# Second attention layer of a hybrid decoder step: 33 steps of one or two units, products ordered by shape

## The chip, the cores and the metric

The kernel runs on one core of one Trainium2 chip. The time of a kernel is the device time of one execution in microseconds; the figure used is the median over several runs. A profiled execution gives a page and a trace; its time is one single value and is told beside its span.

The engines named below are TensorE (PE; loading of its weights is listed as PEld), VectorE (DVE), ScalarE (ACT), GpSimd (POOL) and SyncE (SP). Every large load of the part that is changed is issued by SP, in one queue and in the order in which the instructions stand there.

## The reference

One inference step of a small decoder with two layers: a prompt of 512 positions and eight sequences of four new positions each. All is float32.

```python
D_MODEL = 1024; SEQ = 512; DEC_BATCH = 8; DEC_SEQ = 4; PAST_LEN = 1024
KV_HEADS = 8; ATT_HEAD_DIM = 128
WINDOWS = (128, 512, 2048); DILATIONS = (1, 4, 16)
...
u = rmsnorm(h, g_norm) @ w_in                      # second layer: queries of 3 groups x 8 heads, and the gate
q = u[..., :Q_WIDTH].reshape(b, l, N_DIL_GROUPS, KV_HEADS, ATT_HEAD_DIM)
for g in range(N_DIL_GROUPS):                      # one attention for each dilation group
    o, lse = attend(q[:, :, g], biases[g], DILATIONS[g], WINDOWS[g] // DILATIONS[g])
w = jax.nn.softmax(jnp.stack(lses, axis=0), axis=0)
o = jnp.sum(w[..., None] * jnp.stack(outs, axis=0), axis=0)
y = o.reshape(b, l, ATT_WIDTH) * jax.nn.silu(gate)
return y @ w_out
```

The first layer is a state-space mixer (a projection to 5,152 columns, a short convolution, a scan over chunks of 128 positions, a gate and an output projection). From its result one set of keys and values is projected. The second layer attends with three dilations. The prompt's queries attend within the prompt; the new positions attend to 1,024 cached positions and their own four, with the cached keys and values read from memory. A last norm follows.

## The kernel before, in words

The kernel is one program with five stretches: the first mixer, its output projection with the projection of keys and values, the second layer's attention, the output projection, and the last norm. The attention stretch runs from about 570 us to 875 us of the span, and the change is in it alone.

**Weight products.** A float32 product is made of three products of halves: weights and data are each split into a high and a low part, and high by high, high by low and low by high are summed. In the attention stretch the generator `filler()` hands out weight products one by one: the projection to queries and gates (tiles `pa` and `pb`, from data `bq` and weights `whi` and `wlo`, 128 by 128 weights, 272 columns wide; twelve of them make one block), 1,344 in all, and then those of the output projection. Every one of them uses all 128 columns of TensorE. `run(n)` takes the next n. ACT makes `whi` and DVE makes `wlo` from the loaded `wraw`, three blocks ahead.

**Attention units.** `attend(h, n)` is head h and block n of 128 prompt queries; `sample(h, q)` is head h and four of the eight sequences. Each is a generator, cut by `yield` into stages. There are eight heads with four blocks and two samples each, and `combine()`, which weighs the new positions' three groups.

`attend` has four stages. The first forms scores `sp` in PSUM: eight products with 32 columns for the dilated groups and one full product, then the bias and the exponential on DVE and ACT. The second turns the weights (`ptp`, two or three full transposes) and copies them out (`pt`, `ptz`, on ACT). The third forms `pv`: one or two full products and four with 32 columns; ACT scales it. The fourth turns the result (`op`, one full transpose).

`sample` has three stages. The first loads the bias (`sbt`, four loads, with the head's first sample), loads the cached keys (`kc`, two loads of 640 KB into a tile with two buffers), forms scores `s` from them with products of 32 columns (first `s1`, four products 512 wide, of which the first two read the first load of `kc`; then `s2`), runs the softmax into `ss`, and issues the loads of the cached values (`vc`, two of 640 KB, two buffers). The second loads the new values (`vn`), turns `ss` (`w`: six full transposes into two PSUM tiles) and copies it to `wt` on ACT. The third forms `so`: twenty products of 32 columns with `vc` and four with `vn`.

A load into `kc` waits until the `s` that reads the buffer's former content is done, a load into `vc` until the `so` of the sample before is done. All of these PSUM tiles but `pa` and `pb` share one tag with five buffers (`pss`).

**What sets the order.** The program order of TensorE's instructions is kept as written. The other engines' instructions, SP's loads among them, are put in order by the scheduler, and each engine works its list in that order. The written order of the attention stretch is the loop at lines 1643 to 1668: 49 units in a row. An iteration runs the next stage of units u−4, u−2 and u−3, then starts unit u, then takes 24 weight products (20 from unit 44 on). A unit's stages are thus spread over up to five iterations, with weight products between.

Of the kernel before, what the change touches and what calls it, by code (L numbers as in the profile page):

```python
# [34 lines left out]
ATH = 8  # L35
# [19 lines left out]
OCN, SKIP = 2, 1  # L55
POOL_A = (0, 1, 2, 3)
POOL_B = (0, 1, 2)
PRO, OFF, PACE = 9, 8, (57, 62, 64, 44)
LA, FILL, SLOW = 2, (24, 20), 44
TH = T // 2  # L60


# [65 lines left out]
def tile_yoco_step(  # L128
# [16 lines left out]
    def mm(*a, **k):  # L145
        pin(nc.tensor.matmul(*a, **k))  # L146
# [147 lines left out]
    def dap(t, off, ap):  # L294
        a = t[:]
        return bass.AP(tensor=a.tensor, offset=a.offset + off, ap=ap)
# [617 lines left out]
    live = []  # L914
# [457 lines left out]
    def attend(h, n):  # L1372
        bt, qp = bt_t[h], [qp_t[h, g] for g in range(3)]
        kv = kv_t[h]
        kt = kv[:, 0, :]
        vb, vr = (kv[:, i, 0:SEQ].rearrange("p (n d) -> p n d", n=4) for i in (1, 2))
        kp = kt[:, NS:T]
        ktr = kp.rearrange("p (n r i) -> p r n i", n=4, r=4)
        bt12 = bt[:, 256:512].rearrange("p (a c) -> p a c", a=2)
        w = 32 * (n + 1)  # L1380
        g0 = 128 if n == 0 else 256
        sp = pss("sp")
        k0 = max(0, n - 1) * 128
        for g in range(2):
            for r in range(4):
                mm(sp[32 * r:32 * r + 32, g0 + w * g:g0 + w * g + w],
                   qp[1 + g][:, 128 * n + 32 * r:128 * n + 32 * r + 32], ktr[:, r, 0:n + 1, :], start=True, stop=True)
        mm(sp[:, 0:g0], qp[0][:, 128 * n:128 * n + 128], kp[:, k0:128 * n + 128], start=True, stop=True)
        s_ = wk.tile([128, 512], F32, name="s", bufs=3)
        mx = wk.tile([128, 4], F32, name="mx", bufs=4)  # L1390
        s12 = s_[:, g0:g0 + 2 * w].rearrange("p (a c) -> p a c", a=2)
        nc.vector.tensor_tensor_reduce(out=s12, in0=sp[:, g0:g0 + 2 * w].rearrange("p (a c) -> p a c", a=2),
                                       in1=bt12[:, :, 128 - w:128], scale=1.0, scalar=-3e38,
                                       op0=ALU.add, op1=ALU.max, accum_out=mx[:, 1:2])
        nc.vector.tensor_tensor_reduce(out=s_[:, 0:g0], in0=sp[:, 0:g0], in1=bt[:, 256 - g0:256], scale=1.0,
                                       scalar=-3e38, op0=ALU.add, op1=ALU.max, accum_out=mx[:, 0:1])
        nc.vector.tensor_scalar(mx[:, 2:3], mx[:, 0:1], mx[:, 1:2], -1.0, op0=ALU.max, op1=ALU.mult)
        nc.scalar.activation(s_[:, 0:g0 + 2 * w], s_[:, 0:g0 + 2 * w], AF.Exp, bias=mx[:, 2:3], accum_out=mx[:, 3:4])
        nc.vector.tensor_tensor(s12[:, 0, :], s12[:, 0, :], s12[:, 1, :], op=ALU.add)
        nc.vector.reciprocal(mx[:, 3:4], mx[:, 3:4])  # L1400
        yield
        tp = pss("ptp", (128, 3, 128))
        nk = g0 // 128
        for i in range(nk):
            transpose(tp[:, i, :], s_[:, 128 * i:128 * i + 128], ident)
        transpose(tp[0:w, 2, :], s_[:, g0:g0 + w], ident)
        pt = wk.tile([128, 2, 128], F32, name="pt", bufs=2)
        nc.scalar.copy(pt[:, 0:nk, :], tp[:, 0:nk, :])
        nc.scalar.copy(ptz[n][0:w, :], tp[0:w, 2, :])
        yield  # L1410
        pv = pss("pv")[:, 0:128]
        for i in range(nk):
            b = n - nk + 1 + i
            mm(pv, pt[:, i, :], vb[:, b, :], start=i == 0, stop=False, skip_group_check=True)
        for r in range(4):
            mm(pv[32 * r:32 * r + 32, :], ptz[n][:, 32 * r:32 * r + 32], vr[:, r, :],
               start=False, stop=True, skip_group_check=True)
        on = wk.tile([128, 128], F32, name="on", bufs=1)
        nc.scalar.activation(on, pv, AF.Copy, scale=mx[:, 3:4])
        yield  # L1420
        if h not in op_t:
            op_t[h] = pss("op")
        op = op_t[h]
        transpose(op[:, 128 * n:128 * n + 128], on, ident)
        op_n[h] = op_n.get(h, 0) + 1
        yt = y_t[h // 4][:, h % 4, :]
        if h == 7 and op_n[h] >= 3:
            c0, c1 = ((128, SEQ), (0, 128))[op_n[h] - 3]
            y7 = yt[:, NS + c0:NS + c1]
            assert len(gated) == 2  # L1430
            nc.vector.scalar_tensor_tensor(y7, op[:, c0:c1], 0.5, y7, op0=ALU.mult, op1=ALU.mult)
            y_split(h, NS + c0, NS + c1)
        elif h < 7 and op_n[h] == 4:
            nc.vector.tensor_copy(yt[:, NS:T], op)
            att_done.add(h)
# [5 lines left out]
    def sample(h, q):  # L1441
# [27 lines left out]
        for jp in range(2):  # L1469
            vc.append(wk.tile([128, 2, 5, 128], F32, name="vc", bufs=2))  # L1470
            dma(vc[jp], cv[h, q, :, 2 * jp:2 * jp + 2, :, :])
        yield
        dma(vn[0:TS], dap(vnd, h * 128 + 4 * q * TS * ATH * 128, [[ATH * 128, TS], [TS * ATH * 128, 4], [1, 128]]))
        w1, w2 = pss("w1", (128, 4, 128)), pss("w2", (128, 2, 128))
        for i in range(5):
# [2 lines left out]
        nc.scalar.copy(wt[:, 0:4, :], w1)  # L1478
        nc.scalar.copy(wt[:, 4, :], w2[:, 0, :])
        nc.scalar.copy(wt[0:TS, 5, :], w2[0:TS, 1, :])  # L1480
        yield
        so = pss("so")[:, 0:128]
        for i in range(6):
# [6 lines left out]
    def combine():  # L1490
# [16 lines left out]
        with tc.high_priority():  # L1507
# [7 lines left out]
                nc.vector.tensor_tensor(lgv[:, g], lgv[:, g], sm_, op=ALU.mult)  # L1515
            nc.vector.memset(lt[:, :, 12:32], 0.0)
        yield
        lp2 = pss("lp2")
        transpose(lp2[:, 0:16], lt.rearrange("p a b -> p (a b)"), ident[0:16, 0:16])
        cmw = sbt[:, 0:272].rearrange("p (a b) -> p a b", b=16)  # L1520
        ws, cm = cmw[:, 16, :], cmw[:, 0:16, :]
        with tc.high_priority():
            nc.vector.tensor_copy(ws, lp2[:, 0:16])
            nc.vector.tensor_tensor(cm, sel[:, None, :].to_broadcast([128, 16, 16]), bc(ws, 16), op=ALU.mult)
        yield
        oc = pss("oc", (128, ATH, 2, 16))
        for h in range(ATH):
# [108 lines left out]
    def run(n):  # L1636
        m = min(n, ahead[0]) if n > OCN else 0
        ahead[0] -= m
        for _ in range(n - m):
            if next(fill, 0) == 0:  # L1640
                return

    units = [(f, (h, i)) for h in range(ATH - 1) for f, i in
             ((attend, 0), (sample, 0), (attend, 1), (attend, 2), (sample, 1), (attend, 3))]
    units += [(sample, (7, 0)), (attend, (7, 1)), (attend, (7, 2)), (sample, (7, 1)), (attend, (7, 3)), (combine, ()), (attend, (7, 0))]
    fill = filler()
    fetch_kv(0)
    for _ in range(2 * 84):
        next(fill)
    fetch_kv(1)  # L1650
    live = []
    for u in range(len(units) + LA + 2):
        i = u - LA
        if u == len(units) - 2 + SKIP:
            ahead[0] = ATH * OCN
        for j in (i - 2, i, i - 1):
            if 0 <= j < len(units):
                next(live[j], 0)
        if u < len(units):
            f, a = units[u]  # L1660
            if f is attend and a[0] not in bt_t:
                bt_t[a[0]] = bias_tile(a[0])
            if f is attend and a[1] == 2 and 0 < a[0] < ATH - 1:
                fetch_kv(a[0] + 1)
            live.append(f(*a))
            next(live[u])
        run(FILL[u >= SLOW])
    run(10000)
    bctx.close()

# [94 lines left out]
```

## Time and profile before

| | |
|---|---|
| median of 3 runs | 926.12 us (924.83 to 927.18) |
| profiled execution | 932.11 us, span 930.2 us |
| granted TensorE clock, mean | 0.996 |
| TensorE busy | 908.9 us, 98% of the span |
| VectorE, ScalarE, GpSimd busy | 74%, 53%, 18% |
| attention stretch | about 570 to 875 us of the span |
| cached keys and values | 32 + 32 loads of 640 KB each on SP's queue |

A row of the timeline gives start and length in us, the engine, the line, and what was formed from what; several instructions in a row of one kind are put together, and a product of 32 columns stands in it as `128*32` and counts two records. The start of the next row tells when TensorE took up the next thing; the lengths overlap, since products are pipelined. Numbers after `[` are the idle time just before and what ended it. Line 146 is the helper for all products, line 149 that for all transposes, so groups are told apart by their tiles.

### The profile page before, as it was taken

What the parts mean: (1) busy time and instruction counts of PE and PEld (TensorE: products, weight loads), DVE (VectorE), ACT (ScalarE), POOL (GpSimd) and SP (SyncE); (2) the same over time, 40 slices, a digit from 0 to 9 for tenths busy, and PEclk for the clock granted to TensorE, in tenths of its full rate; (3) what the DMA queues carried; (4) which work ended last, traced back from release to release, by engine and by line L of the source; (5) the groups of instructions that cost most, each with busy time, mean ns of one, the idle gap of its engine ahead of it and who ended that gap; (6) DMA issues with size and microseconds to landing.
All of it is one profiled execution on the core that took longest, in us unless ns stands there. A gap on an engine that the chain in (4) does not pass through costs nothing.

```text
span 930.2 us, 21888 instructions
## 1 busy us (share of the span) xinstructions
PE 908.9 (98%) x8671; PEld 847.9 (91%) x8671; DVE 687.5 (74%) x1435; ACT 489.9 (53%) x1140; POOL 163.0 (18%) x212
## 2 busy tenths in 40 slices
PE   8999999999999999999999999999999999999997
PEld 7989888888989889999999999999899999989997
DVE  6998899989799899644489335876677766778732
ACT  6678655655566655422255213555455555557642
POOL 2031344433514642111101001000000000000021
PEclk9999999999999999999999999999999999999999
DMA  8224365355364442536277556757768868774511
GB/s 295 93 74 155 104 206 166 121 170 170 134 201 161 149 165 101 156 108 228 90 256 227 183 184 196 265 182 264 252 203 262 280 204 267 270 256 155 194 49 49
DMA packets 80573, 168.48 MB, mean 181 GB/s; under 512 B 19990, under 2 KB 37736, under 8 KB 79960
## 3 DMA queue, kind: packets, MB, share of 16 engines
q1 hardware_dynamic: 73784, 154.60, 50.5%
q10 hardware_dynamic: 5616, 9.75, 2.8%
q0 software_dynamic: 1072, 2.74, 1.1%
q8 instruction: 68, 1.11, 0.5%
q14 instruction: 33, 0.27, 0.1%
HBM read 141.14 MB, written 25.93 MB: 180 GB/s over the span
## 4 chain that ended last, share of the span: by engine, by line
PE 82%; DVE 9%; DMA 4%; ACT 2%; issue 2%; POOL 0%; SPq 0%; POOLq 0%; DVEq 0%; ACTq 0%
PE pa L146 33%; PE pb L146 28%; PE sp L146 3%; PE pv L146 2%; PE so L146 2%; PE s L146 2%; DVE wlo L206 2%; DMA kc<-ck 1%; PE yd L146 1%; DMA m<-aed 1%; DVE co L641 1%; PE csp L146 1%; PE w L149 1%; PE ptp L149 1%; PE xp L149 1%
## 5 line engine op out<-in xcount | busy, mean ns | idle before, releaser
L205 ACT ACTIVATE whi<-wraw 128x1024 fp32r<-128x1024 f32 x69 | 72.8, 1056 | 97.0 <-PE pb L146 57.2
L206 DVE TENSOR_TENSOR wlo<-wraw,whi 128x1024 fp32r<-128x1024 f32 x69 | 89.6, 1298 | 45.1 <-ACT whi L205 44.7
L146 PE MATMUL pa<-bq,whi 128*128 128x272 f32 x512 | 103.1, 296 | 0.0
L146 PE MATMUL pb<-nl,whi 128*128 128x288 f32 x280 | 84.0, 300 | 0.0
L146 PE MATMUL pb<-nh,wlo 128*128 128x288 f32 x280 | 83.5, 298 | 0.0
L146 PE MATMUL pb<-nh,whi 128*128 128x288 f32 x280 | 83.4, 298 | 0.0
L146 PEld LDWEIGHTS pa<-bq,whi 128*128 128x128 f32 x512 | 81.2, 189 | 0.9
L146 PE MATMUL pa<-nh,whi 128*128 128x256 f32 x280 | 81.1, 290 | 0.5 <-DVE uz L681 0.5
L146 PE MATMUL pa<-nl,whi 128*128 128x256 f32 x280 | 80.7, 288 | 0.0
L146 PE MATMUL pa<-nh,wlo 128*128 128x256 f32 x280 | 80.1, 286 | 0.0
L146 PE MATMUL pb<-bq,whi 128*128 128x272 f32 x384 | 77.2, 296 | 1.3 <-DVE kv L1230 1.1
L146 PE MATMUL pa<-bq,wlo 128*128 128x272 f32 x256 | 74.2, 290 | 0.0
L641 DVE SCALAR_TENSOR_TENSOR co<-cb,cvp,co 128x568 f32<-128x568 f32 x72 | 64.0, 892 | 1.5 <-ACT co L639 0.9
L146 PEld LDWEIGHTS pb<-bq,whi 128*128 128x128 f32 x384 | 60.8, 189 | 2.6 <-DVE kv L1230 1.3
L1289 ACT ACTIVATE whi<-wraw 128x512 fp32r<-128x512 f32 x64 | 40.1, 627 | 35.2 <-PE pb L146 16.8
L146 PEld LDWEIGHTS pb<-nl,whi 128*128 128x128 f32 x280 | 53.0, 189 | 4.4 <-issue 4.4
L146 PEld LDWEIGHTS pa<-nh,whi 128*128 128x128 f32 x280 | 53.8, 192 | 2.6 <-issue 1.9
L146 PE MATMUL pb<-bq,wlo 128*128 128x272 f32 x192 | 55.5, 289 | 0.0
L146 PEld LDWEIGHTS pa<-nl,whi 128*128 128x128 f32 x280 | 53.8, 192 | 1.4 <-issue 1.4
L146 PEld LDWEIGHTS pb<-nh,wlo 128*128 128x128 f32 x280 | 53.1, 190 | 2.2 <-issue 2.2
L146 PEld LDWEIGHTS pa<-nh,wlo 128*128 128x128 f32 x280 | 53.8, 192 | 0.9 <-issue 0.9
L146 PEld LDWEIGHTS pb<-nh,whi 128*128 128x128 f32 x280 | 53.0, 189 | 0.8 <-issue 0.8
(408 smaller groups left out, 2788.0 us busy)
## 6 DMA issues: line engine op xcount, KB each, us to landing
wraw<-w_in SPq DMA_DIRECT2D x40, 512.0 KB
kc<-ck SPq DMA_DIRECT2D x32, 640.0 KB
vc<-cv SPq DMA_DIRECT2D x32, 640.0 KB
wraw<-wb SPq DMA_DIRECT2D x32, 512.0 KB
s<-s SPq DMA_DIRECT2D x32, 256.0 KB
m<-aed SPq DMA_DIRECT2D x16, 512.0 KB
ssmS<-s ACTq DMA_DIRECT2D x32, 256.0 KB
wraw<-w_out SPq DMA_DIRECT2D x16, 512.0 KB
```

The lines of the kernel that those rows point to most:

```text
L146: pin(nc.tensor.matmul(*a, **k))
L149: pin(nc.tensor.transpose(*a))
L205: a = nc.scalar.activation(hi, raw, AF.Copy)
L206: b = lo_eng.tensor_tensor(lo, raw, f32(hi), op=ALU.subtract)
L641: nc.vector.scalar_tensor_tensor(o, cb[:, k:k + n], cvp[:, ti, k:k + 1], o, op0=ALU.mult, op1=ALU.add)
L1289: nc.scalar.activation(hi, src[p][j], AF.Copy)
```

## The change

The 49 units become 33 steps of one or two units: for each head (first sample, block 0), (block 1), (second sample, block 2), (block 3), and a tail for the last head with `combine` and a last block. Each stage that mixes shapes gets one more `yield`, so that a step can run the full products of several units first, then all products with 32 columns, then the full score products. A step u runs the transposes of step u−4, those of u−2, the full `pv` of u−3, then the 32-column products of u−3 (`so`, `pv`) and of the new step u (`s`, `sp`), then the full `sp`, then 36 weight products (40, 24 and 40 in three late steps, 20 after them). The weight products of a head are 144 in both versions (6 × 24 and 4 × 36).

```diff
@@ -56,7 +56,7 @@
 POOL_A = (0, 1, 2, 3)
 POOL_B = (0, 1, 2)
 PRO, OFF, PACE = 9, 8, (57, 62, 64, 44)
-LA, FILL, SLOW = 2, (24, 20), 44
+LA = 2
 TH = T // 2
 
 
@@ -1385,6 +1385,7 @@
             for r in range(4):
                 mm(sp[32 * r:32 * r + 32, g0 + w * g:g0 + w * g + w],
                    qp[1 + g][:, 128 * n + 32 * r:128 * n + 32 * r + 32], ktr[:, r, 0:n + 1, :], start=True, stop=True)
+        yield
         mm(sp[:, 0:g0], qp[0][:, 128 * n:128 * n + 128], kp[:, k0:128 * n + 128], start=True, stop=True)
         s_ = wk.tile([128, 512], F32, name="s", bufs=3)
         mx = wk.tile([128, 4], F32, name="mx", bufs=4)
@@ -1412,6 +1413,7 @@
         for i in range(nk):
             b = n - nk + 1 + i
             mm(pv, pt[:, i, :], vb[:, b, :], start=i == 0, stop=False, skip_group_check=True)
+        yield
         for r in range(4):
             mm(pv[32 * r:32 * r + 32, :], ptz[n][:, 32 * r:32 * r + 32], vr[:, r, :],
                start=False, stop=True, skip_group_check=True)
@@ -1470,6 +1472,7 @@
             vc.append(wk.tile([128, 2, 5, 128], F32, name="vc", bufs=2))
             dma(vc[jp], cv[h, q, :, 2 * jp:2 * jp + 2, :, :])
         yield
+        yield
         dma(vn[0:TS], dap(vnd, h * 128 + 4 * q * TS * ATH * 128, [[ATH * 128, TS], [TS * ATH * 128, 4], [1, 128]]))
         w1, w2 = pss("w1", (128, 4, 128)), pss("w2", (128, 2, 128))
         for i in range(5):
@@ -1478,6 +1481,7 @@
         nc.scalar.copy(wt[:, 0:4, :], w1)
         nc.scalar.copy(wt[:, 4, :], w2[:, 0, :])
         nc.scalar.copy(wt[0:TS, 5, :], w2[0:TS, 1, :])
+        yield
         yield
         so = pss("so")[:, 0:128]
         for i in range(6):
@@ -1515,6 +1519,7 @@
                 nc.vector.tensor_tensor(lgv[:, g], lgv[:, g], sm_, op=ALU.mult)
             nc.vector.memset(lt[:, :, 12:32], 0.0)
         yield
+        yield
         lp2 = pss("lp2")
         transpose(lp2[:, 0:16], lt.rearrange("p a b -> p (a b)"), ident[0:16, 0:16])
         cmw = sbt[:, 0:272].rearrange("p (a b) -> p a b", b=16)
@@ -1522,6 +1527,7 @@
         with tc.high_priority():
             nc.vector.tensor_copy(ws, lp2[:, 0:16])
             nc.vector.tensor_tensor(cm, sel[:, None, :].to_broadcast([128, 16, 16]), bc(ws, 16), op=ALU.mult)
+        yield
         yield
         oc = pss("oc", (128, ATH, 2, 16))
         for h in range(ATH):
@@ -1640,31 +1646,39 @@
             if next(fill, 0) == 0:
                 return
 
-    units = [(f, (h, i)) for h in range(ATH - 1) for f, i in
-             ((attend, 0), (sample, 0), (attend, 1), (attend, 2), (sample, 1), (attend, 3))]
-    units += [(sample, (7, 0)), (attend, (7, 1)), (attend, (7, 2)), (sample, (7, 1)), (attend, (7, 3)), (combine, ()), (attend, (7, 0))]
+
+
+    steps = [[(f, (h, i)) for f, i in st] for h in range(ATH - 1) for st in
+             (((sample, 0), (attend, 0)), ((attend, 1),), ((sample, 1), (attend, 2)), ((attend, 3),))]
+    steps += [[(sample, (7, 0)), (attend, (7, 1))], [(attend, (7, 2))], [(sample, (7, 1)), (attend, (7, 3))],
+              [(combine, ())], [(attend, (7, 0))]]
+    fills = [36] * (4 * (ATH - 1)) + [40, 24, 40]
     fill = filler()
     fetch_kv(0)
     for _ in range(2 * 84):
         next(fill)
     fetch_kv(1)
     live = []
-    for u in range(len(units) + LA + 2):
-        i = u - LA
-        if u == len(units) - 2 + SKIP:
+    for u in range(len(steps) + LA + 2):
+        if u == len(steps) - 2 + SKIP:
             ahead[0] = ATH * OCN
-        for j in (i - 2, i, i - 1):
-            if 0 <= j < len(units):
-                next(live[j], 0)
-        if u < len(units):
-            f, a = units[u]
-            if f is attend and a[0] not in bt_t:
-                bt_t[a[0]] = bias_tile(a[0])
-            if f is attend and a[1] == 2 and 0 < a[0] < ATH - 1:
-                fetch_kv(a[0] + 1)
-            live.append(f(*a))
-            next(live[u])
-        run(FILL[u >= SLOW])
+
+        for j in (u - LA - 2, u - LA, u - LA - 1, u - LA - 1):
+            if 0 <= j < len(steps):
+                for g_ in live[j]:
+                    next(g_, 0)
+        if u < len(steps):
+            for f, a in steps[u]:
+                if f is attend and a[0] not in bt_t:
+                    bt_t[a[0]] = bias_tile(a[0])
+                if f is attend and a[1] == 2 and 0 < a[0] < ATH - 1:
+                    fetch_kv(a[0] + 1)
+            live.append([f(*a) for f, a in steps[u]])
+
+            for _ in range(2):
+                for g_ in live[u]:
+                    next(g_, 0)
+        run(fills[u] if u < len(fills) else 20)
     run(10000)
     bctx.close()
 
```

TensorE's list around a first sample of a head, in the kernel before (the last head but one; `pb` is the first of the weight products, the rest of which are left out):

```order
L149 MATMUL op<-ident,on 128x128
L149 MATMUL ptp<-ident,s 128x128 x3
L146 MATMUL so<-vc,wt 32x128 x20
L146 MATMUL so<-vn,wt 32x128 x4
L146 MATMUL s_10413<-kc,qpad_7031 32x512 x4
L146 MATMUL s_10414<-kc,qpad_7031 32x128 x4
L146 MATMUL s_10414<-kv,qpad_7031 32x4 x4
L146 MATMUL pb<-bq_6918,whi 128x272 x2
...
L149 MATMUL ptp<-ident,s 32x128
L146 MATMUL pv<-kv,pt 128x128 x2
L146 MATMUL pv<-kv,ptz_7038 32x128 x4
L146 MATMUL sp<-kv,qp 32x64 x8
L146 MATMUL sp<-kv,qp 128x256
```

Two iterations are seen, each with one run of 32-column products: the value and score products of two samples in the one, the `pv` and `sp` of blocks in the other.

The same place in TensorE's list of the changed kernel, one step with a sample, from its first transpose to its full score product:

```order
L149 MATMUL op<-ident,on 128x128
L149 MATMUL w_10533<-ident,ss 128x128 x4
...
L149 MATMUL w_10534<-ident,ss 4x128
...
L149 MATMUL ptp<-ident,s 32x128
L146 MATMUL pv<-kv,pt 128x128 x2
L146 MATMUL pv<-kv,ptz_7038 32x128 x4
L146 MATMUL s_10566<-kc,qpad_7031 32x512 x4
L146 MATMUL s_10567<-kc,qpad_7031 32x128 x4
L146 MATMUL s_10567<-kv,qpad_7031 32x4 x4
L146 MATMUL sp<-kv,qp 32x96 x8
L146 MATMUL sp<-kv,qp 128x256
```

All full transposes and full `pv` products now stand ahead of one run of 32-column products, in which `pv`, `s` and `sp` follow each other. `so` stands in the steps without a new sample, and the 36 weight products follow the full `sp`. Over the stretch the runs of 32-column products between full ones are 51 before and 35 after.

SP's list around a head's first key load in the kernel before (`bt` is the bias of the prompt's blocks; `kc` in the fifth row holds the first keys of a head, `vc` behind it the first values of the same head):

```order
L1366 DMA bt<-bvd 32x8x32
L1368 DMA bt<-bvd 32x2x128
L196 DMA wraw<-wb 128x1024
L1439 DMA sbt<-bsd 12x644 x4
L1450 DMA kc<-ck 128x1280 x2
L1471 DMA vc<-cv 128x1280 x2
L196 DMA wraw<-wb 128x1024
L1473 DMA vn<-vnd 4x4x128
L1189 DMA kv<-kvd 128x544
```

Here the key load stands ahead of the value load, with only the bias and a weight load ahead of both.

The same place of the changed kernel:

```order
L1366 DMA bt<-bvd 32x8x32
L1368 DMA bt<-bvd 32x2x128
L1441 DMA sbt<-bsd 12x644 x3
L1473 DMA vc<-cv 128x1280 x2
L1476 DMA vn<-vnd 4x4x128
L1441 DMA sbt<-bsd 12x644
L1452 DMA kc<-ck 128x1280 x2
L196 DMA wraw<-wb 128x1024 x2
```

The value load of the head before (second sample), its `vn` and the last bias load now stand ahead of the next head's first key load. This is so at the first sample of heads 1 to 7. At the second sample of heads 1, 4 and 5 the second key load stands behind a value load as well.

## The prediction

> **What bounds the kernel now.** I read the page's busy shares first, then its chain of waits, then windows over the second layer, then the timelines of TensorE and of SP's queue in it.
>
> ```profile
> PE 908.9 (98%) x8671; PEld 847.9 (91%) x8671; DVE 687.5 (74%) x1435; ACT 489.9 (53%) x1140; POOL 163.0 (18%) x212
> PE 82%; DVE 9%; DMA 4%; ACT 2%; issue 2%; POOL 0%; SPq 0%; POOLq 0%; DVEq 0%; ACTq 0%
> 650.00:700.00 50.00, 48.95 (x640) 43.91 (x638) 33.97 (x103) 26.11 (x73) 0.55 (x3) 1.00 0.72 230
> 700.00:750.00 50.00, 50.00 (x656) 45.80 (x656) 37.45 (x117) 28.32 (x77) 1.34 (x3) 1.00 0.81 267
> 791.16 3.01 PE pa L146 x24
> ```
>
> TensorE is busy 98% of the span and is 82% of the chain that ends last. The windows list span, then busy time of PE, weight loads, DVE, ACT and POOL, granted clock, DMA share and GB/s: in the changed stretch TensorE has next to no gap (48.95 and 50.00 of 50 us) at a clock of 1.00, DVE works 71% and the DMA engines 77%. So this stretch ends when TensorE has put its list through, and a gain must shorten that list; a loss must open gaps in it. The chain row prices a weight product: 24 in 3.01 us, 0.1254 each.
>
> **What the change removes.** Products and their number stay; the switches between 128-column and 32-column products fall. Counted in TensorE's order, excursions out of the full shape and back are 51 before and 35 after: 16 fewer (per head six become four, over eight heads). The price of one is read here (start, us; a 32-column product shows as two records):
>
> ```profile
> 678.93 0.49 PE L149 MATMUL ptp<-ident,s 128*128 128x128 f32 x3
> 679.36 1.30 PE L146 MATMUL so<-vc,wt 128*32 128x128 f32 x40
> 680.69 1.26 PE L146 MATMUL s<-kc,qpad 128*32 128x512 f32 x16
> 681.77 0.22 PE L146 MATMUL s<-kv,qpad 128*32 128x4 f32 x8
> 681.92 0.52 PE L146 MATMUL pb<-bq,whi 128*128 128x272 f32 x2
> 682.28 0.29 PE L146 MATMUL pb<-bq,wlo 128*128 128x272 f32 x1
> 690.23 0.27 PE L149 MATMUL op<-ident,on 128*128 128x128 f32 x1
> 690.34 0.82 PE L149 MATMUL w<-ident,ss 128*128 128x128 f32 x6
> 690.99 0.61 PE L146 MATMUL pv<-kv,pt 128*128 128x128 f32 x4
> 691.53 0.43 PE L146 MATMUL pv<-kv,ptz 128*32 128x128 f32 x8
> 691.78 0.73 PE L146 MATMUL sp<-kv,qp 128*32 128x32 f32 x18
> ```
>
> Going in: six full transposes start in 690.34 to 690.99, 0.108 each, so three should give way after 0.33, but so starts 0.43 after ptp: 0.10 lost. Four full pv records take 0.54 up to the 32-column pv, against 0.44: 0.10 again. Coming out: the first two weight products take 0.36 (681.92 to 682.28) against 0.25, 0.11 lost, and of the 0.15 between 681.77 and 681.92 I put 0.06 to the four narrow products and 0.09 to the switch. Together 0.30 us; without the 0.09 it is 0.21, and with both entries' rounding 0.35. So 16 × 0.30 = **4.8 us** off (3.4 to 5.6).
>
> **What it moves: the queue.** All loads of this stretch stand in order on SP's queue. Each sample has four large ones: two halves of the cached keys, kc, and two of the cached values, vc, 640 KB each. A vc load can only go out when so has read the values of the sample before.
>
> ```profile
> 629.14 0.80 SPq L1471 DMA_DIRECT2D vc<-cv  x2
> 630.75 1.36 SPq L1450 DMA_DIRECT2D kc<-ck  x2
> 656.36 0.84 SPq L1450 DMA_DIRECT2D kc<-ck  x2
> 680.68 0.80 SPq L1471 DMA_DIRECT2D vc<-cv  x2
> 691.04 0.83 SPq L1450 DMA_DIRECT2D kc<-ck  x2
> 697.21 0.80 SPq L1471 DMA_DIRECT2D vc<-cv  x2
> 697.22 1.26 PE L146 MATMUL s<-kc,qpad 128*32 128x512 f32 x16
> ```
>
> Rows: issue, us, line, load. Before, most key loads go well ahead of need: kc goes at 691.04, its s starts at 697.22 without a gap. In the changed order the first key load of a head h stands right behind vc, vn and one or two sbt of the head before; vc waits for so, now in step 4h−1, and the keys are wanted by s in step 4h. That holds for seven heads (1 to 7). Queued behind the waiting vc are vn, sbt, kc and the next weights; only s is close to its need, the weights have half a step and more.
>
> The time from the one to the other, from starts above and these:
>
> ```profile
> 685.03 0.49 PE L149 MATMUL ptp<-ident,s 128*128 128x128 f32 x3
> 685.36 0.61 PE L146 MATMUL pv<-kv,pt 128*128 128x128 f32 x4
> 686.14 1.25 PE L146 MATMUL sp<-kv,qp 128*32 128x128 f32 x18
> 687.10 0.53 PE L146 MATMUL pb<-bq,whi 128*128 128x272 f32 x2
> ```
>
> vc goes out 1.32 after so's start (679.36 to 680.68), which is so's end. Then come the 32-column pv 0.25 (691.53 to 691.78), sp 0.96 (686.14 to 687.10) and 36 weight products, 36 × 0.1254 + 0.11 = 4.62: 5.83 to the end of step 4h−1. In step 4h there stand before s: op 0.11, w 0.65, ptp 0.33 (685.03 to 685.36), pv 0.54, its 32-column part 0.25: 1.88. From vc's issue to s that is 5.83 + 1.88 = 7.7 us. The second half of the keys is read by the third product of s only, where in the trace it was late once (last row below: a gap of 0.42 ended by kc, s itself having begun at 662.84); the two products ahead of it are a third of the 1.2 us of s (680.69 to 681.92), 0.4. So in **8.1 us** must land vc, vc, kc, kc: 2.62 MB.
>
> ```profile
> 680.68:681.64 0.96, 0.96 (x20) 0.36 (x16) 0.93 (x3) 0.37 (x1) 0.00 (x0) 1.00 0.00 0
> 681.64:686.12 4.48, 4.48 (x59) 4.34 (x55) 2.78 (x9) 2.41 (x6) 0.18 (x1) 1.00 0.96 318
> 629.14:636.88 7.74, 7.74 (x101) 6.85 (x94) 5.50 (x17) 3.57 (x10) 0.58 (x1) 1.00 0.91 324
> 697.21:704.95 7.74, 7.74 (x101) 6.85 (x94) 5.52 (x18) 3.51 (x9) 0.18 (x1) 1.00 0.91 276
> 656.81 7.46 DMA kc<-ck
> 662.84 1.05 PE L146 MATMUL s<-kc,qpad 128*32 128x512 f32 x4 [0.63 <-DMA kc<-ck]
> 664.31 0.62 PE L146 MATMUL s<-kc,qpad 128*32 128x512 f32 x6 [0.42 <-DMA kc<-ck]
> ```
>
> After the issue of a vc pair nothing moves for 0.96 us (first row), then 318 GB/s (second). At that pace four loads need 0.96 + 2.62 MB / 318 GB/s = 0.96 + 8.24 = 9.2 us. At the 276 GB/s of the fourth row, where other loads share the engines, it is 0.96 + 9.49 = 10.5. With 324 GB/s from the first moment on, as in the third row, where transfers were under way already, 8.1. I take 9.5: near the first, since in the new order only vn and sbt, small ones, stand between, and a little above it, since weights run on. That s does wait on a late key load the chain shows: 7.46 us from a second half's issue to its landing, on the path. So the wait is 9.5 − 8.1 = **1.4 us**, between 0.0 and 2.4. 7 × 1.4 = **9.8 us** on (0 to 16.8).
>
> The Trainium skill, "DMA: Bandwidth & Descriptors", section "Anatomy of one DMA — SWDGE (gpsimd) path", fits a transfer's time as about 2.0 us plus its bytes over 436 GB/s. It is stated for another path than SP's; taken for the four loads as one it gives, as an estimate, 2.0 + 6.0 = 8.0 us, hence no wait at all in place of 9.8 (and none of the 0.6 below): 920 us. The pair at 680.68 moved at 318, not 436, so the trace speaks against it.
>
> The second half of the keys of a head's second sample stands behind a vc that waits for three heads (1, 4, 5): one load fewer in the same window, 0.96 + 1.97 / 0.318 = 7.1 us against 8.1, or 8.1 at 276 GB/s; with weights and kv between them, up to 0.8 each, I take 0.2: **0.6 us** on (0 to 2.4).
>
> ```profile
> L146 PE MATMUL s<-kc,qpad 128*32 128x512 f32 x128 | 19.2, 594 | 1.4 <-DMA kc<-ck 1.4
> L1478 ACT COPY wt<-w 128x512 f32<-128x512 f32 x16 | 9.3, 580 | 0.0
> L1289 ACT ACTIVATE whi<-wraw 128x512 fp32r<-128x512 f32 x64 | 40.1, 627 | 35.2 <-PE pb L146 16.8
> L1290 DVE TENSOR_TENSOR wlo<-wraw,whi 128x512 fp32r<-128x512 f32 x64 | 44.0, 688 | 7.2 <-ACT whi L1289 6.5
> L146 PE MATMUL pb<-bq,whi 128*128 128x272 f32 x384 | 77.2, 296 | 1.3 <-DVE kv L1230 1.1
> ```
>
> The waits for keys that TensorE has now, **1.4 us** (first row), belong to an order that no longer exists: off.
>
> **What I cost at nothing.** The extra PSUM tiles: a step with a sample now asks for op, w1, w2, ptp, pv, s1, s2 and sp of five buffers, so s1 needs an early one copied out. The wt copy takes 0.58 (second row); it can start when w is done, 0.76 into the step, and would be done at 1.34, 0.5 before s at 1.88. ACT is free half of the time; the cover is that half us, and a cast of 0.63 just ahead of the copy (third row) would eat it and 0.1 more. Each further piece of that size that ACT does first would put 0.6 on the path. Weight products 36 in a row, 4.6 us, against 3.1: their weights' low halves come from DVE at 0.69 for 12 products (fourth row), so 36 need 2.1 us of DVE's time in 4.6, and DVE is at 71% over the whole; the share of weight products in the time is unchanged, so the mean is covered. The tail after the last head, where weight products wait 1.1 us for DVE's kv (last row), I leave as it is (±1).
>
> **The sum**, against the profiled execution of 932.11 us (span 930.2): 932.1 − 4.8 − 1.4 + 9.8 + 0.6 = 936.3. That execution stood 6.0 above the median of the runs, 926.12, so the time is 936.3 − 6.0 = **930 us**.
>
> **The rivals.**
>
> A, the forecast: keys land late, 930; its own range is 925 to 936, from 0.7 to 2.2 a head.
>
> B, the keys land in time, faster: it decides where four loads take less than 8.1 us, 324 GB/s from the issue on. For it: that rate was reached over 7.74 us with transfers under way (third row), and between the four little else is queued. Against it: the 0.96 of stillness after an issue that had waited. Then 932.1 − 4.8 − 1.4 − 6.0 = 920. The Trainium skill's fit, named above, falls here.
>
> C, buffers: ACT is late with the copies of w, since two casts of 0.63 and not one stand ahead, and s waits for its PSUM tile in the 16 steps with a sample, whether or not its keys are there. It decides when a copy is over 0.5 late. For it: seven or eight tiles in five buffers. Against: ACT at 54% in the windows. Price 16 × 0.6 = 9.6 where keys are in time, 920 + 9.6 = 930, slower than before though the keys are not late; on top of late keys only the other 9 steps count, 930 + 5 = 935.
>
> D, the switches cost nothing that the order can save (the time is the products' own after all): then A without the 4.8, 935. Against it: the same 0.10 stands in two places of two kinds.
>
> **How the numbers follow.** A 0.52, B 0.26, C 0.14, D 0.08. What this kernel's runs can tell from no change is about 0.3%, 2.8 us: no change is 923.3 to 928.9. B lies below that but for waits of a few tenths; A with 1.2 us a head or less lies within it (0.2 less on each of seven takes 1.4 off 930); the rest of A, C and D above. Faster 0.27, within 0.22, slower 0.51. The range is 920 to 938: it leaves out the lower part of B (0.12), where nothing waits at all and the switches are worth more, and A, C and D near their upper bounds (0.08).
>
> **What would show it.** Right: in the changed profile s has idle time ahead of it of about 10 us in all, released by kc, in seven places some 34 us apart (four steps), each behind a vc issue that follows so; the chain shows kc rows of 5 to 7 us; the switch-in rows are fewer with the same 0.10 each; DVE and ACT waits of TensorE unchanged. Wrong: s starts without a gap though kc goes out behind vc (B; look at GB/s from the vc issue on, above 324); or the gap ahead of s is released by ACT's wt (C); or weight products wait for wlo within the rows of 36, which I cost at nothing and would add to any of them.

## The result, and the profile after

The changed kernel is slower: 940.58 us (median of 6 runs, 938.71 to 942.75) against 927.36 (6 runs, 924.83 to 927.85), a ratio of 1.0149 with a 95% interval of 1.013 to 1.0167, or 13.2 us. Forecast were 930 us, with a range of 920 to 938. The sign and the place were forecast; the size was not.

The page of the changed kernel (busy shares, and the chain by engine), then the same two windows of the second layer as before, then two of TensorE's waits (us in all, times, longest):

```profile
PE 912.3 (97%) x8671; PEld 848.8 (90%) x8671; DVE 686.7 (73%) x1435; ACT 489.0 (52%) x1140; POOL 161.0 (17%) x212
PE 71%; DVE 11%; DMA 10%; ACT 3%; issue 3%; SPq 1%; POOL 0%; DVEq 0%; POOLq 0%; ACTq 0%
```

```profile
650.00:700.00 50.00, 47.27 (x572) 42.30 (x571) 31.85 (x99) 25.64 (x71) 0.95 (x3) 1.00 0.81 263
700.00:750.00 50.00, 49.17 (x639) 43.95 (x638) 36.02 (x117) 27.09 (x74) 0.55 (x3) 1.00 0.66 218
```

```profile
PE s L146 <- DMA kc<-ck: 7.4, 12, 1.8
PE lp L149 <- DVE lse L1496: 1.5, 1, 1.5
```

TensorE's share of the chain fell from 82% to 71%, and transfers rose from 4% to 10%. Fewer products went through in the same window (640 before, 572 now, in the first), at the same clock of 1.00. The wait for the keys is now TensorE's longest, 7.4 us in 12 places against 1.4 in three; lp did not wait before.

One of the seven places, the first sample of head 3: SP's timeline, TensorE's timeline (rows between them left out), and, from the chain, its rows for keys (start, us, what).

```profile
684.04 0.83 SPq L1473 DMA_DIRECT2D vc<-cv  x2
684.97 0.28 SPq L1476 DMA_DIRECT2D vn<-vnd  x1
685.30 0.32 SPq L1441 DMA_DIRECT2D sbt<-bsd  x1
685.67 1.04 SPq L1452 DMA_DIRECT2D kc<-ck  x2
```

```profile
682.71 1.30 PE L146 MATMUL so<-vc,wt 128*32 128x128 f32 x40
689.87 0.27 PE L149 MATMUL op<-ident,on 128*128 128x128 f32 x1
691.50 0.42 PE L146 MATMUL pv<-kv,ptz 128*32 128x128 f32 x8
691.86 1.05 PE L146 MATMUL s<-kc,qpad 128*32 128x512 f32 x4
693.34 0.62 PE L146 MATMUL s<-kc,qpad 128*32 128x512 f32 x6 [0.43 <-DMA kc<-ck]
693.79 0.71 PE L146 MATMUL s<-kc,qpad 128*32 128x512 f32 x4
694.44 0.18 PE L146 MATMUL s<-kv,qpad 128*32 128x4 f32 x2
```

```profile
615.07 8.08 DMA kc<-ck
651.32 8.07 DMA kc<-ck
686.07 7.22 DMA kc<-ck
720.43 6.88 DMA kc<-ck
737.15 7.41 DMA kc<-ck
755.83 7.03 DMA kc<-ck
790.02 8.31 DMA kc<-ck
825.27 7.01 DMA kc<-ck
```

The value load goes out at 684.04, 1.33 after so began; sbt and the keys go out only behind it. s would have followed pv at 691.74, 7.70 us after that issue: the window was forecast right. The second half of the keys ends the chain row at 686.07 + 7.22 = 693.29, and s goes on at 693.34. The chain has such a row for the first sample of each head from 1 to 7, some 35 us apart, and one more at the second sample of head 4 (737.15).

The page counts only time in which TensorE did nothing at all, and that undercounts here. In the kernel before, all of s takes 1.1 us from its first product to the start of its last, narrow ones (680.69 to 681.77). Here two products begin at 691.86, and from 693.34, when the second half is there, s still takes 1.1 us, to its last ones at 694.44. So what is late is all of s, and I count as **lateness** the time from when s would have started to the start of the first product that reads the second half: 693.34 − 691.74 = 1.6 us here. Worked out in this way from the trace's records for each of the 16 samples:

```
                      vc issue   end of chain row   after issue   lateness
head 1, first sample   612.96        623.15            10.19        2.55
head 2                 648.20        659.39            11.19        3.54
head 3                 684.04        693.29             9.25        1.60
head 4                 717.92        727.31             9.39        1.74
head 5                 753.31        762.86             9.55        1.90
head 6                 787.91        798.33            10.42        2.77
head 7                 822.98        832.28             9.30        1.65
sum of the seven                                                   15.75
the other nine samples                                              2.83
all, changed kernel                                                18.58
all, kernel before, this trace and a second one              4.27, 2.29
```

**The account.** The stretch from the first weight product of the second layer to the last op took 302.9 us before and 312.8 after: 9.9 more. Lateness makes 18.6 − 4.3 = 14.3 of it, lp's wait 1.6, and a wait of a weight product in the tail became 0.5 shorter (1.2 to 0.7; these two, too, are counted from when the product would have started, some 0.1 more than the page's idle time). What is left over, 9.9 − 14.3 − 1.6 + 0.5 = −5.5 us, I put down to the order by shape; the experiments price it a second way.

### The profile page after: what moved, and what is told of

It is laid out like the page before. It is cut to its first block, busy times and chain, and to the rows that moved or that the text cites. A ratio compares the mean times of both kernels' runs of the same rounds, so it can differ in the third digit from the quotient of the medians.

```text
span 938.9 us, 21872 instructions
## 1 busy us (share of the span) xinstructions
PE 912.3 (97%) x8671; PEld 848.8 (90%) x8671; DVE 686.7 (73%) x1435; ACT 489.0 (52%) x1140; POOL 161.0 (17%) x212
## 4 chain that ended last, share of the span: by engine, by line
PE 71%; DVE 11%; DMA 10%; ACT 3%; issue 3%; SPq 1%; POOL 0%; DVEq 0%; POOLq 0%; ACTq 0%
PE pa L146 29%; PE pb L146 25%; DMA kc<-ck 6%; PE so L146 2%; PE sp L146 2%; PE s L146 2%; DVE wlo L206 2%; DMA m<-aed 2%; PE pv L146 2%; DVE vl L875 1%; DVE co L641 1%; PE yd L146 1%; PE csp L146 1%; PE xp L149 1%; PE ptp L149 1%
```

## The experiments

A run of the kernel before stands beside each; ratios are to it.

**Keys ahead of the values.** The next sample's key loads are written ahead of this sample's value loads (`nx` is the next sample; `load_keys` holds the two loads that stood in `sample`, and is left out here).

```diff
...
+        nx = (h + q, 1 - q)
+        if nx[0] < ATH:
+            kc_t[nx] = load_keys(*nx)
         vc = []
         for jp in range(2):
             vc.append(wk.tile([128, 2, 5, 128], F32, name="vc", bufs=2))
```

> The changed kernel, with the next sample's two key loads written ahead of the value loads of the sample before it, so that they no longer stand behind a load that waits for so. Theory A (late keys): in the changed trace the keys were late by 18.6 us in all, of which none should be left; 940.6 - 18.6 = 922 us (920 to 925), under the kernel before by some 5, and s starts without idle time released by kc. Rival C (PSUM buffers, or 36 products in a row): the queue is not the cause, still over 935. Rival D (the switches are worth nothing): the keys are in time, but no gain is left, 926 to 929.

Measured: 944.67 us, ratio 1.017 (1.0145 to 1.0195). The lateness fell from 18.6 to 0.8 us, as expected, but the time did not fall to 922. TensorE's waits in this kernel, and SP's timeline some 14 us ahead of the longest of them (at 814.6):

```profile
PE pb L146 <- ACT whi L1289: 6.5, 3, 4.6
PE pb L146 <- DVE wlo L1290: 3.1, 4, 1.1
PE lp L149 <- DVE lse L1504: 2.7, 1, 2.7
```

```profile
799.86 0.81 SPq L1481 DMA_DIRECT2D vc<-cv  x2
800.77 1.12 SPq L196 DMA_DIRECT2D wraw<-wb  x2
```

Now weights stand behind the value load that waits for so (800.77, right behind 799.86), and whi and wlo come late; from this list alone, that the one makes the other is read, not shown. SP waited 79.0 us for so in this kernel, 51.8 in the changed one. So the keys' wait was removed and another put in its place by the same list: the experiment shows that the keys' place made them late, and does not show what the change is worth without that.

The waits are not the whole loss here. The granted clock was 1.00 through the whole stretch in the changed kernel; in this trace it was 0.50 for 3.4 us from 688.8, for 6.8 us from 815.1 (below) and for 3.4 us from 862.9, each time beginning about 1 us or less after a wait of TensorE had ended.

```profile
815.10:821.90 6.80, 6.18 (x28) 6.14 (x28) 2.12 (x6) 1.54 (x3) 0.00 (x0) 0.50 0.42 132
```

As an estimate, 13.6 us at half the clock cost up to 6.8 us, beside the 12.3 us of the three waits listed. That the waits bring the lower clock is read from the order in time, not shown: the longest wait for keys in the changed kernel, 1.8 us, had no such stretch behind it.

**The same edit in the kernel before.**

> The kernel before, with the same edit alone: key loads ahead of the value loads in SP's list, 49 units as before. In the one trace of before the keys were late by 4.3 us in all (two places), elsewhere not. Theory A: at most those 4.3 go, 923 to 927. It gives the kernel to which the order by shape is compared with the keys in time in both: keys_first should then lie about 5 us under it by the switches (16 x 0.3), and level with it by rival D.

Measured: 946.50 us, ratio 1.021 (1.0184 to 1.0235): the expectation failed. Lateness 0.3 us, but transposes wait for the exponentials of both kinds of unit:

```profile
PE ptp L149 <- ACT s L1398: 9.2, 5, 3.7
PE w L149 <- ACT ss L1470: 3.0, 2, 1.6
```

The order of 49 units, too, loses some 19 us when this one list is put in another order; up to 5 of them, as an estimate, go to 10.2 us of the stretch at a clock of 0.50. It is no clean base for the comparison I wanted, and what exactly stood behind what here I did not follow further.

**Weight products moved ahead, 50 and 22.**

```diff
+    for k in range(1, ATH):
+        fills[4 * k - 1] += 14
+        fills[4 * k] -= 14
```

> The changed kernel with 14 weight products moved from the step of a head's first sample (36 to 22) to the step ahead of it (36 to 50), for heads 1 to 7; the queue as in the change. Theory A: the time from the value load's issue to s grows by 14 x 0.1254 = 1.76 us, so the lateness of the seven loads (2.6, 3.5, 1.6, 1.7, 1.9, 2.8, 1.7) falls to 0.8, 1.8, 0, 0, 0.1, 1.0, 0: 12 us less, 928 to 930 us. Rival C: longer rows of weight products make it worse or leave it, 940 or more.

Measured: 942.74 us, ratio 1.0161 (1.014 to 1.0183); lateness 22.9 us in all, 7.2 of it at head 3. The edit moved loads in SP's list as well: at head 3 a weight load that waits for DVE now stands between the values and the keys, and the keys go out at 686.34, 6.8 us after vc (1.6 in the change):

```profile
679.54 0.83 SPq L1473 DMA_DIRECT2D vc<-cv  x2
684.20 0.33 SPq L196 DMA_DIRECT2D wraw<-wb  x1
686.34 0.83 SPq L1452 DMA_DIRECT2D kc<-ck  x2
```

At head 6 a weight load came between them too, at heads 4 and 7 two more bias loads. Where the list up to the keys stayed as it was, at heads 1, 2 and 5, the lateness fell from 2.55, 3.54 and 1.90 to 0.65, 1.09 and 0.02: by 1.9 to 2.5 for a window that is 1.76 longer, as it should be if the keys' landing is what s waits for. The time of the whole says nothing on the window, since the other heads did not keep the rest.

**Weight products moved ahead, 40 and 32.** The same with 4. The list up to the keys stays at six of the seven heads; at head 6, against what was expected, a weight load came between the values and the keys here too.

> The changed kernel with only 4 weight products moved to the step ahead of a head's first sample (40 and 32 in place of 36 and 36, heads 1 to 7). The trial with 14 moved the loads about in SP's list, so that it tested another order; with 4 the list around kc and vc stays as it is in the change. Theory A: the time from the value load's issue to s grows by 4 x 0.1254 = 0.5 us, and the lateness of the keys of each of seven heads falls by as much, from 2.25 to 1.75 on the mean, 3.5 us in all; 937 us. If something else than the landing sets s (a PSUM buffer, the steps), the lateness stays at 2.25 and the time at 940 to 941.

Measured: 941.38 us, ratio 1.014 (1.012 to 1.0159), lateness 21.1 us. The window grew as worked out: at head 3 vc goes at 682.05 and s would have begun at 690.26, 8.21 us later, not 7.70. But the last packet of the keys landed 10.0 us after vc's issue on the mean of the seven heads, not 9.5, so that the mean lateness was 2.36, not 1.75. My expectation missed: a longer window was eaten by later landings. Two heads make up most of that: head 6, where the keys go out 2.40 us after vc and not 1.63 (late by 3.40, 2.77 in the change), and head 3, where the list is the same and the chain row ends 11.26 us after the issue, not 9.25 (late by 3.10, not 1.60). At the other five the mean lateness fell from 2.28 to 2.01. Within the changed kernel's one trace the landings differ by 2 us from head to head, so that one trace of each cannot settle half a microsecond. It is the landing all the same that releases s (12 places and 7.4 us in the change, 13 and 8.5 here).

**GpSimd issues the value loads.** The waiting loads leave SP's queue.

```diff
-            dma(vc[jp], cv[h, q, :, 2 * jp:2 * jp + 2, :, :])
+            nc.gpsimd.dma_start(vc[jp], cv[h, q, :, 2 * jp:2 * jp + 2, :, :])
...
-        dma(vn[0:TS], dap(vnd, ...))
+        nc.gpsimd.dma_start(vn[0:TS], dap(vnd, ...))
```

> The changed kernel with the value loads (vc, vn) issued by GpSimd, whose queue holds nothing else that is urgent; on SP's queue no load stands behind one that waits for so any more, neither keys nor weights. In the run with the keys merely put ahead, the keys were in time but weights stood behind the waiting vc instead (TensorE waited 6.5 us for whi, 3.1 for wlo). Theory A (what matters is which load stands behind the one that waits for so): no waits for kc, whi or wlo, 940.6 - 18.6 = 922 us, between 919 and 926. Rival E (the loads of a head together are too much for the pace that the steps set, whatever their order): waits for kc or weights stay, over 935. Rival C (buffers, long rows of products): over 935 with waits for ACT or DVE.

Measured: 927.27 us (12 runs), ratio 0.9993 (0.9972 to 1.0013), with no wait for keys or weights on TensorE worth a row; s now waits in two places for something else:

```profile
PE s L146 <- ACT wt L1481: 1.8, 2, 1.5
PE lp L149 <- DVE lse L1496: 1.5, 1, 1.5
```

Of the change's 13.2 us all are gone, but 922 was not reached. The stretch took 297.8 us in this trace, 15.0 less than in the changed kernel and 3.4 and 5.1 less than in the two traces of before. Two things hold the rest: s is late by 2.2 us in two places, now for wt, and the end of the kernel became longer. Behind TensorE's last product stand 8.2 us here, 6.1 in the changed kernel. Most of the 8.2 is a DRAIN of GpSimd, with 0.8 us behind it. The rows give the shortest, the median and the longest DRAIN in ns, in the changed kernel and in this one:

```profile
L1775 POOLq DRAIN  x3: 46/106/2984, 933.4 to 938.6; - x3
L1775 POOLq DRAIN  x3: 46/98/6911, 914.3 to 921.8; - x3
```

So 940.6 − 15.0 + 2.2 = 927.8, and 927.27 was measured.

**The same edit in the kernel before.**

> The kernel before with the same edit alone: value loads issued by GpSimd. Theory A: its late keys (4.3 us in the one trace) go, 923 to 927. vc_pool then lies 5 us under it by the switches alone (16 x 0.30), level with it if switches are worth nothing.

Measured: 931.84 us (12 runs), ratio 1.0038 (1.0021 to 1.0056), slower than before by 3.1 us (928.72 in the runs beside it), against the expectation. The stretch took 302.9 us, as in the first trace of before; 2.2 of the 3.1 lie behind the last product, where GpSimd's DRAIN takes 6.9 us here too. vc_pool lies 4.6 us under this kernel by the medians and 5.1 by the stretch (302.9 and 297.8): that is what the new order is worth with the value loads out of SP's list in both, where 5 were expected.

**Order by shape undone, twice.** Each unit's stage runs in one piece; steps and fills stay. The edit stands once on top of the keys-first kernel (unsorted) and once on top of vc_pool.

```diff
-        for j in (u - LA - 2, u - LA, u - LA - 1, u - LA - 1):
-            if 0 <= j < len(steps):
-                for g_ in live[j]:
-                    next(g_, 0)
+        for j, m in ((u - LA - 2, 1), (u - LA - 1, 2), (u - LA, 1)):
+            if 0 <= j < len(steps):
+                for g_ in live[j]:
+                    for _ in range(m):
+                        next(g_, 0)
...
-            for _ in range(2):
-                for g_ in live[u]:
+            for g_ in live[u]:
+                for _ in range(2):
                     next(g_, 0)
```

> keys_first with the order by shape undone and all else kept, steps, fills and queue: in a step op, then so, then pv full and 32-column, then w and ptp, then s, then sp 32-column and full, each unit in one piece. Excursions to 32 columns 80, not 35. By the price of 0.30 us read before, 45 x 0.30 = 13.5 us over keys_first (at 0.21: 9.5); by rival D no difference.

Measured: 960.42 us, ratio 1.0353 (1.0328 to 1.0377), 15.8 over keys_first, or 0.35 for each of 45 excursions, with late weights in both, and with 13.6 and 17.1 us at a clock of 0.50; the next pair had a clock of 1.00 through the whole stretch.

> vc_pool with each unit's stage run in one piece in a step: 80 excursions to 32 columns, not 35; steps, fills and queues as in vc_pool. At 0.30 us each 13.5 us over vc_pool (9.5 at 0.21); if switches are worth nothing, level with it. The pair keys_first and unsorted stood 15.8 apart, but both waited for weights.

Measured: 937.55 us, ratio 1.0100 (1.0069 to 1.0130), 10.3 over vc_pool: 0.23 each. By the traces, with lateness and lp's wait taken off both stretches (309.3 − 2.0 − 0.9 and 297.8 − 2.5 − 1.6), 12.7 us: 0.28 each. So a switch costs 0.23 to 0.28 us here and rival D falls; the entry alone takes 0.205 from a full product to a 32-column one, in these traces too, where the next full one takes 0.11.

**GpSimd issues the key loads instead.**

```diff
-            dma(kc[jp], ck[h, q, :, 2 * jp:2 * jp + 2, :])
+            nc.gpsimd.dma_start(kc[jp], ck[h, q, :, 2 * jp:2 * jp + 2, :])
```

> The changed kernel with the key loads, not the value loads, issued by GpSimd: the keys leave SP's list, where all else keeps its place behind the value load as in the change. Theory A (the loss is the place of the keys behind the value load, nothing else of SP's list): 940.6 - 18.6 = 922 (920 to 926), below vc_pool (0.9993 of the kernel before), in which the weights' place changed too. If keys or weights are late by the sum of all traffic, late s or whi stays, 930 or more.

Measured: 926.49 us (12 runs), ratio 0.9991 (0.9976 to 1.0006). The keys leave SP's list, the weights stay behind the value load, and the whole loss of the change is given back (the bias loads now stand ahead of the value load as well; no row of TensorE's waits is for them). That it would be 922, and less than vc_pool, did not come true. The stretch took 298.7 us, 14.1 less than in the changed kernel; at the end the DRAIN takes 5.6 us, and 7.2 us stand behind the last product. s waits 2.9 us for wt:

```profile
PE s L146 <- ACT wt L1481: 2.9, 3, 1.2
PE lp L149 <- DVE lse L1496: 1.5, 1, 1.5
```

**The tail.** In both kernels with a load on GpSimd, the last long steps take 40, 12, 52 weight products in place of 40, 24, 40.

> vc_pool with 12 weight products of the tail moved from the step after the last sample's to the one ahead of the combination of the groups (40, 12, 52 in place of 40, 24, 40), so that lse is done when lp is due (lp waited 1.5 us for it in the changed kernel and in vc_pool, not before). Expected 1.5 us under vc_pool, whose median was 0.9993 of the kernel before; 0.998 of it, unless the short step of 12 opens another wait.

Measured: 926.69 us (12 runs), ratio 0.9992 (0.9977 to 1.0006), no difference from vc_pool: lp no longer waits, pb waits 1.3 us for DVE's qp (0.6 there).

> kc_pool with 40, 12, 52 weight products in the last three long steps in place of 40, 24, 40. In vc_pool this took the wait of lp for lse away in the trace (1.5 us) but not in the median (0.9993 and 0.9992). 1 to 2 us under kc_pool, or no difference where another wait of the tail (weight products for DVE's qp or kv) takes its place.

Measured: 925.33 us (12 runs), ratio 0.9975 (0.9960 to 0.9989): 2.1 us under the kernel before, and the only version whose interval lies below it; the 1.2 us to kc_pool are less than the spread of either. What it has left is s waiting for a copy of ACT, in TensorE's timeline and among its waits:

```profile
750.75 0.42 PE L146 MATMUL pv<-kv,ptz 128*32 128x128 f32 x8
752.99 1.28 PE L146 MATMUL s<-kc,qpad 128*32 128x512 f32 x16 [1.81 <-ACT wt L1481]
```

```profile
PE s L146 <- ACT wt L1481: 3.3, 4, 1.8
```

**The kernel before once more.**

> The kernel before, unchanged, once more with a profile. In its first trace the keys were late by 4.3 us in all at two places and the execution stood 4.8 us above the median of six. Theory A: those are the same microseconds, so an execution near 927 shows next to no late keys (under 1.5 us), and a slow one some again. If the excess lies in the first layer alone, the lateness is 4 us here too.

Measured: 928.51 us in the one run, lateness 2.3 us, where 1.5 at most was expected for such a time; the second layer began at 569.6 us, not 571.7, and its stretch took 301.2 us, not 302.9. So of the 3.6 us between the two executions 2.1 lie ahead of the second layer and 1.7 in its stretch, about what the late keys differ by (2.0); behind it the second trace took 0.2 more.

## Why the prediction was wrong, by its own steps

The mechanism was right: the keys land late behind the waiting value load, in the seven places named, and the switches are worth what was said. What failed are two ends of the keys' term, 0.4 us each in each of seven places, and the base from which the sum was counted, 6.0 us.

**The switches: right.** 4.8 us off, bounds 3.4 to 5.6. Measured: 5.5 as what the account leaves over, 4.6 and 5.1 by the pair with the value loads on GpSimd. At 0.23 to 0.28 a switch, 16 of them make 3.7 to 4.5.

**The window and the queue: right.** 7.7 us from vc's issue to s, 7.70 found; keys behind vc at the first samples of heads 1 to 7, late in all seven.

**"In 8.1 us must land vc, vc, kc, kc": wrong, and the first half of the miss.** I took 0.4 off the wait since only the third product of s reads the second half of the keys. In the trace's records the first four products of s start within 0.02 us of each other (680.690 to 680.710) and their second passes 0.41 later, together. They run side by side, and the two that could start early only ran ahead alone: from the second half's coming, s took as long as ever, 1.1 us. The window ends at 7.7, with nothing hidden.

**"I take 9.5": the landing right, its end missed.** The last packet landed 9.47 us after vc's issue on the mean of the seven. But s starts 0.4 after that (692.93 and 693.34 at head 3), and the release is what counts: by the chain rows 9.9. So 9.9 − 7.7 = 2.2 a head, measured 2.25, for the 1.4 of the prediction: 15.75 for 9.8. Of these 6 us, half belongs to each of the two errors. The sum of bounds (0 to 16.8) held it, the range did not.

**The other samples:** the second samples of heads 1, 4 and 5 were late by 0.43, 1.35 and 0.43, 2.2 us for 0.6, inside the bounds (0 to 2.4). The nine samples together have 2.8: the rest is mostly the very first sample of all, 0.45, where no value load stands ahead of the keys; the sum has no term for it.

**The waits for keys that exist: sized by idle time.** The row of idle time gave 1.4; by lateness it was 4.3, for the same reason as above.

**The tail, left at ±1:** lp waited 1.6 us for lse, which I had not named; with pb's wait 0.5 shorter, +1.1.

**"So the time is 936.3 − 6.0": wrong, and the second half of the miss.** The terms, with what was measured, give 932.1 − 5.5 − 4.3 + 18.6 + 1.6 − 0.5 = 942.0 (the 5.5 is what the account left over, so this restates it; with the 4.6 to 5.1 of the pair it is 942.4 to 942.9); the profiled execution took 940.69, with 1.9 us less ahead of the second layer. That is 0.1 from its median, 940.58. I had taken the 6.0 us by which one execution of before stood above its median as belonging to both kernels. They belonged to that execution, as far as the second trace of before can tell: in part late keys, which I then took off a second time as a term, in part the first layer. Against 936.3 the result is out by 4.3; against 930 by 10.6.

**The rivals.** B (keys in time): no, the four loads took 8.9 to 10.7 us to the last packet at all seven heads, over the 8.1 at which B began. D (switches worth nothing): no, by the order undone. C (PSUM buffers): not in the changed kernel, where no wait of s for ACT has a row; it stands behind the late keys, for as soon as those are in time, s waits 1.8 to 3.3 us for wt. I had called it an alternative, and it is the next thing in line. Long rows of weight products cost nothing: with the keys out of the way 36 in a row run without a wait for whi or wlo. The estimate from the Trainium skill, "DMA: Bandwidth & Descriptors", "Anatomy of one DMA — SWDGE (gpsimd) path", 8.0 us for the four loads, was too early by 1.5 to the last packet and by 1.9 to the release.

**What stays open:** why the landing at head 3 moved out by 2 us when 4 products were moved; and the last microsecond by which the kernel before is slower with its value loads on GpSimd. In that trace DVE's sums of weights waited 14.1 us for wraw, against 2.2 in the same window of before, but the stretch took the 302.9 us of the first trace of before, so that no cost of this is seen.

## What to carry to other kernels

Before an order is written anew, look at what stands behind each load that waits in the queue, and compare its need with the moment at which the wait ends: with the keys behind a waiting load they came 18.6 us late in all (2.3 to 4.3 before), and the order saved 4.6 to 5.5. Moving a load in one in-order queue moved the wait to what then stood behind it; taking it to a queue of its own removed it, for 0.9 to 2.2 us at the end of the kernel. And take the distance of a profiled execution from its median off the changed kernel only where the view shows that both have it.

## What the runs showed of the hardware

**A transfer ends with its slowest part.** Most of the four loads was there long before the last of it. At head 2, from vc's issue, in two windows (the last two columns are DMA share and GB/s):

```profile
648.20:656.76 8.56, 7.88 (x92) 7.22 (x84) 5.95 (x15) 5.32 (x16) 0.00 (x0) 1.00 0.96 337
656.76:658.92 2.16, 1.00 (x4) 0.17 (x4) 0.00 (x0) 0.00 (x0) 0.00 (x0) 1.00 1.01 402
```

In 8.56 us 337 GB/s make 2.88 MB, of which 0.44 MB are other loads by the trace's packets; nine tenths of the four loads had ended by then. The keys were complete only at 658.92, and in those last 2.2 us the engines moved 402 GB/s, 0.87 MB, of which 0.68 MB are other loads. By the packets, nine tenths of the four loads had ended 7.8 to 8.6 us after the issue at all seven heads, the last packet at 8.9 to 10.7. A rate gives when the bulk is there; what waited for the last packet waited 0.9 to 2.2 us more than for nine tenths.

**Products side by side.** Late data for two of four products that run side by side cost all four: what had run early gave nothing back, for s took 1.1 us from the late data on, as it does with no data late. TensorE's idle time showed 7.4 us of it, lateness 18.6.

**Loads issued by GpSimd are paid for at the end.** GpSimd's long DRAIN at the kernel's end took 2.98 us with the 17 loads that GpSimd issues in the changed kernel, 5.59 with 49 (kc_pool) and 6.91 with 65 (vc_pool); that comes to 0.08 us for each load more. From TensorE's last product to the end the kernel took 6.1, 7.2 and 8.2 us.
